# A two-layer ReGLU MLP on one core: x through a DRAM copy and transposing loads, weights in smaller loads, warm-up matmuls ahead

## The chip, the cores and the metric

One core of one Trainium2 chip runs the kernel. The metric is the device time in microseconds (us). Engines are named as the profile names them: PE is TensorE (PEld its weight loads), DVE VectorE, ACT ScalarE, POOL GpSimd, SP SyncE. POOL and SP issue the DMAs; POOL's queue is q0, SP's is q1.

## The reference

```python
def reference(x, w1, w2):          # x [16, 256, 512], w1 [512, 4096], w2 [2048, 512], all fp32
    h = x @ w1
    gate, value = np.split(h, 2, axis=-1)
    h = np.maximum(gate, 0) * value
    return (h @ w2).astype(np.float32)
```

## The kernel before

The 16 x 256 rows of x are 4096 tokens, cut into 8 blocks of 512 (TPB). Blocks are worked in pairs, so there are four passes. All matrix products run in bf16; the weights are cast from fp32 in the DMA that loads them, stay in SBUF for the whole run (w1_sb, w2_sb), and are loaded once, by POOL.

A block needs xT, its x transposed so that the 512 input features lie on the partitions (four slabs of 128, k = 0 to 3). prep_xT makes it. For blocks 0 and 1 (fast_start) SP loads four pieces of 128 tokens in fp32 into x_stage, which has four buffers (L69), an engine that the planner picks casts each to bf16 (L70), TensorE transposes 128 x 128 tiles by a matmul against ident into a PSUM tile ptr (L80), and VectorE copies a finished ptr to xT (L88). For blocks 2 to 7 POOL issues one cast load per block instead of the four pieces (L74); the transposes are the same, 16 a block.

mm1_reglu_pass runs over j, the 16 column tiles of the hidden layer, and inside it over the two blocks of the pair: four matmuls of 512 columns into pv (value half of w1, L113), four into pg (gate half, L121), then ScalarE copies pv to vb (L129) and VectorE forms max(pg, 0) * vb as a slice of h2T (L130). That is 256 matmuls a pass. mm2_pass makes eight output tiles of 128 tokens in a pass, each from 16 matmuls (L145); ScalarE copies the PSUM tile po to ob, of which there are four buffers (L153), and SP stores it (L155). That is 128 matmuls a pass, and none of a pass's mm2 can begin before its h2T slices are there.

w1 is loaded in eight chunks of 512 columns, gate and value halves in turn (L95), each one DMA over all four k; w2 in four groups of four k-tiles (L101). They are traced after the preparation of blocks 0 and 1.

The order of instructions on each engine is fixed when the kernel is built. A planner walks the traced program with a machine model, takes what is ready by the model, and prefers what was traced first; what it puts in a queue is executed in that order, and a head that waits holds the rest of its queue back. The preparation of the next pair is traced ahead of a pass (L171), so the planner may put its transposes among the matmuls of the pass before. Semaphores and buffer reuse are handled by the same layer. At launch, instructions of the launch code (L196, L207) stand around those of the kernel.

Of the kernel before, what the change touches and what calls it, by code (L numbers as in the profile page):

```python
# [10 lines left out]
@with_exitstack  # L11
def kernel(
    ctx: ExitStack,
    tc: tile.TileContext,
    x: bass.AP,
    w1: bass.AP,
    w2: bass.AP,
    out: bass.AP,
):
    nc = tc.nc  # L20
    P = 128
    FP32 = mybir.dt.float32
    BF16 = mybir.dt.bfloat16
    AX = mybir.AluOpType

    x2 = x.flatten_outer_dims()
    out2 = out.flatten_outer_dims()
    M, D = x2.shape
    D_w, H2 = w1.shape
    H, DO = w2.shape  # L30
    assert D_w == D and H2 == 2 * H

    TPB = 512
    NB = M // TPB
    PAIR = 2
    NP = NB // PAIR
    KD = D // P
    NJ = H // P
    KH = H // P
    TS = TPB // P  # L40
    assert NB % PAIR == 0

    consts = ctx.enter_context(tc.tile_pool(name="consts", bufs=1))
    wpool = ctx.enter_context(tc.tile_pool(name="wpool", bufs=1))
    xT_pool = ctx.enter_context(tc.tile_pool(name="xT_pool", bufs=4))
    stage = ctx.enter_context(tc.tile_pool(name="stage", bufs=4))
    h2_pool = ctx.enter_context(tc.tile_pool(name="h2_pool", bufs=4))
    out_pool = ctx.enter_context(tc.tile_pool(name="out_pool", bufs=4))
    psum_mm1 = ctx.enter_context(tc.tile_pool(name="psum_mm1", bufs=2, space=bass.MemoryType.PSUM))
    psum_mm2 = ctx.enter_context(tc.tile_pool(name="psum_mm2", bufs=2, space=bass.MemoryType.PSUM))  # L50
    psum_tr = ctx.enter_context(tc.tile_pool(name="psum_tr", bufs=2, space=bass.MemoryType.PSUM))

    ident = consts.tile([P, P], BF16, name="ident")
    make_identity(nc, ident)

    w1_sb = wpool.tile([P, KD, H2], BF16, name="w1_sb")
    w2_sb = wpool.tile([P, KH, DO], BF16, name="w2_sb")

    w1_r = w1.rearrange("(po pi) f -> pi po f", pi=P)
    w2_r = w2.rearrange("(po pi) f -> pi po f", pi=P)  # L60

    def prep_xT(tb, fast_start):
        x_bf = stage.tile([P, TS, D], BF16, tag="x_bf", name="x_bf", bufs=3)
        if fast_start:
            for t in range(TS):
                tok0 = tb * TPB + t * P
                x_stage = stage.tile([P, D], FP32, tag="x_stage", name="x_stage",
                                     bufs=4)
                nc.sync.dma_start(out=x_stage, in_=x2[tok0:tok0 + P, :])  # L69
                nc.any.tensor_copy(out=x_bf[:, t, :], in_=x_stage)  # L70
        else:
            src = x2[tb * TPB:(tb + 1) * TPB, :].rearrange(
                "(t pi) d -> pi t d", pi=P)
            nc.gpsimd.dma_start(out=x_bf, in_=src)  # L74

        xT = xT_pool.tile([P, KD, TPB], BF16, tag="xT", name="xT")
        for k in range(KD):
            ptr = psum_tr.tile([P, TPB], BF16, tag="ptr", name="ptr")
            for t in range(TS):
                nc.tensor.matmul(  # L80
                    ptr[:, t * P:(t + 1) * P],
                    x_bf[:, t, k * P:(k + 1) * P],
                    ident,
                    is_transpose=True,
                    start=(t == 0),
                    stop=(t == TS - 1),
                )
            nc.vector.tensor_copy(out=xT[:, k, :], in_=ptr)  # L88
        return xT

    W1C = 512
    nchunk_half = H // W1C

    def load_w1_chunk(c):
        nc.gpsimd.dma_start(  # L95
            out=w1_sb[:, :, c * W1C:(c + 1) * W1C],
            in_=w1_r[:, :, c * W1C:(c + 1) * W1C],
        )

    def load_w2_group(g, gsize=4):  # L100
        nc.gpsimd.dma_start(  # L101
            out=w2_sb[:, g * gsize:(g + 1) * gsize, :],
            in_=w2_r[:, g * gsize:(g + 1) * gsize, :],
        )

    def mm1_reglu_pass(pass_blocks, xTs, h2Ts):
        for j in range(NJ):
            for bi, tb in enumerate(pass_blocks):
                xT = xTs[bi]
                pg = psum_mm1.tile([P, TPB], FP32, tag="pg", name="pg")  # L110
                pv = psum_mm1.tile([P, TPB], FP32, tag="pv", name="pv")
                for k in range(KD):
                    nc.tensor.matmul(  # L113
                        pv,
                        w1_sb[:, k, (NJ + j) * P:(NJ + j + 1) * P],
                        xT[:, k, :],
                        start=(k == 0),
                        stop=(k == KD - 1),
                    )
                for k in range(KD):  # L120
                    nc.tensor.matmul(  # L121
                        pg,
                        w1_sb[:, k, j * P:(j + 1) * P],
                        xT[:, k, :],
                        start=(k == 0),
                        stop=(k == KD - 1),
                    )
                vb = stage.tile([P, TPB], BF16, tag="vb", name="vb", bufs=4)
                nc.scalar.copy(out=vb, in_=pv)  # L129
                nc.vector.scalar_tensor_tensor(  # L130
                    out=h2Ts[bi][:, j, :],
                    in0=pg,
                    scalar=0.0,
                    in1=vb,
                    op0=AX.max,
                    op1=AX.mult,
                )

    def mm2_pass(pass_blocks, h2Ts):
        for bi, tb in enumerate(pass_blocks):  # L140
            h2T = h2Ts[bi]
            for t in range(TS):
                po = psum_mm2.tile([P, DO], FP32, tag="po", name="po")
                for k in range(KH):
                    nc.tensor.matmul(  # L145
                        po,
                        h2T[:, k, t * P:(t + 1) * P],
                        w2_sb[:, k, :],
                        start=(k == 0),
                        stop=(k == KH - 1),  # L150
                    )
                ob = out_pool.tile([P, DO], FP32, tag="ob", name="ob")
                nc.scalar.copy(out=ob, in_=po)  # L153
                tok0 = tb * TPB + t * P
                nc.sync.dma_start(out=out2[tok0:tok0 + P, :], in_=ob)  # L155

    xT_tiles = {}
    xT_tiles[0] = prep_xT(0, fast_start=True)
    xT_tiles[1] = prep_xT(1, fast_start=True)

    for c in range(nchunk_half):
        load_w1_chunk(c)
        load_w1_chunk(c + nchunk_half)
    for g in range(KH // 4):
        load_w2_group(g)

    for p in range(NP):
        pass_blocks = [p * PAIR + i for i in range(PAIR)]

        next_blocks = [tb + PAIR for tb in pass_blocks if tb + PAIR < NB]  # L170
        for tb in next_blocks:  # L171
            xT_tiles[tb] = prep_xT(tb, fast_start=False)

        xTs = [xT_tiles.pop(tb) for tb in pass_blocks]
        h2Ts = [
            h2_pool.tile([P, KH, TPB], BF16, tag="h2T", name="h2T")
            for _ in pass_blocks
        ]

        mm1_reglu_pass(pass_blocks, xTs, h2Ts)  # L180
        mm2_pass(pass_blocks, h2Ts)


# [28 lines left out]
```

## Time and profile before

| | us |
|---|---|
| median of 6 runs (370.84 to 373.3) | 372.23 |
| the profiled execution | 370.84 |
| its span, first to last instruction | 369.1 |
| PE busy | 345.1 (94%) |
| DVE busy | 102.8 (28%) |
| ACT busy | 98.7 (27%) |
| POOL busy | 14.2 (4%) |
| mean granted TensorE clock | 0.989 |

The busy share of TensorE counts a matmul from its start to its modelled end, so matmuls that overlap in the pipeline, or run slowly, count as busy all the same. The slices of the page cut the span in 40 pieces of 9.2 us; a digit is a busy share in tenths.

### The profile page before, as it was taken

To read this page: it belongs to the slowest core of one execution; us is meant where nothing else is said; L and a number is where in the kernel's file an instruction comes from. 1 tells how busy PE (TensorE), PEld (TensorE's weight loads), DVE (VectorE), ACT (ScalarE), POOL (GpSimd) and SP (SyncE) were. 2 spreads that over 40 slices of the span, in tenths; PEclk is the share of its full clock that TensorE was granted. 3 is DMA by queue.
4 is the path that set the end of the run, shared out by engine and by line. 5 is a ranking of instruction groups with operands and counts; after the bars stand their busy time and mean duration, and the time that the engine had idled before them with its cause. 6 is when DMAs were issued, how large, how long until landed. Compare 5 with 4: busy or idle time off the path is not lost.

```text
span 369.1 us, 4092 instructions
## 1 busy us (share of the span) xinstructions
PE 345.1 (94%) x1664; PEld 160.0 (43%) x1664; DVE 102.8 (28%) x162; ACT 98.7 (27%) x167; POOL 14.2 (4%) x24
## 2 busy tenths in 40 slices
PE   1597399999999999999999999999999999999996
PEld 0343254444445444444445444444444444444442
DVE  1343153441004443442004433442000433432000
ACT  2233023331112333332112333332112333332111
POOL 7220010000000000000000000000000000000000
PEclk9999699999999999999999999999999999999999
DMA  8999980000215000000221000000212000000212
GB/s 200 250 206 207 206 126 2 1 1 30 85 57 113 2 0 2 0 0 7 80 87 57 0 2 2 0 2 0 85 59 85 0 2 0 0 2 0 85 59 87
DMA packets 15283, 20.19 MB, mean 55 GB/s; under 512 B 928, under 2 KB 10144, under 8 KB 15264
## 3 DMA queue, kind: packets, MB, share of 16 engines
q0 software_dynamic: 9504, 9.44, 15.7%
q1 hardware_dynamic: 5760, 10.49, 7.8%
q8 instruction: 13, 0.21, 0.2%
q14 instruction: 6, 0.05, 0.0%
HBM read 20.97 MB, written 8.39 MB: 80 GB/s over the span
## 4 chain that ended last, share of the span: by engine, by line
PE 87%; DMA 10%; POOL 1%; issue 1%; ACT 0%; POOLq 0%; ACTq 0%
PE po L145 30%; PE pg L121 28%; PE pv L113 28%; DMA x_bf<-in_x_dram 6%; DMA w_sb<-in_w_dram 4%; PE ptr L80 2%; POOL w_sb L95 1%; POOL w_sb L101 0%; ACT ob L153 0%; POOL ident masks.py:199 0%; POOL ident masks.py:197 0%; POOLq masks.py:199 0%; ACTq L153 0%; POOLq L196 0%; POOLq L74 0%
## 5 line engine op out<-in xcount | busy, mean ns | idle before, releaser
L121 PE MATMUL pg<-xT,w_sb 128*128 128x512 bf16 x512 | 134.6, 382 | 0.0
L113 PE MATMUL pv<-xT,w_sb 128*128 128x512 bf16 x512 | 133.7, 382 | 0.0
L130 DVE SCALAR_TENSOR_TENSOR h2T<-pg,vb 128x512 bf16<-128x512 f32 x128 | 88.5, 691 | 155.8 <-PE pg L121 154.7
L129 ACT CAST vb<-pv 128x512 bf16<-128x512 f32 x128 | 74.9, 585 | 161.2 <-PE pv L113 161.2
L145 PE MATMUL po<-w_sb,h2T 128*128 128x512 bf16 x512 | 111.2, 379 | 0.0
L145 PEld LDWEIGHTS <-h2T 128*128 128x128 bf16 x512 | 50.1, 98 | 60.4
L121 PEld LDWEIGHTS <-w_sb 128*128 128x128 bf16 x512 | 50.3, 98 | 58.7 <-issue 0.5
L113 PEld LDWEIGHTS <-w_sb 128*128 128x128 bf16 x512 | 50.2, 98 | 58.4
L153 ACT COPY ob<-po 128x512 f32<-128x512 f32 x32 | 18.7, 585 | 95.4 <-PE po L145 95.4
L80 PE MATMUL ptr<-ident,x_bf 128*128 128x128 bf16 x128 | 15.6, 252 | 20.4 <-ACT x_bf L70 9.3
L88 DVE COPY xT<-ptr 128x512 bf16<-128x512 bf16 x32 | 13.4, 424 | 73.8 <-PE ptr L80 73.3
L80 PEld LDWEIGHTS <-x_bf 128*128 128x128 bf16 x128 | 11.5, 114 | 27.4 <-ACT x_bf L70 10.3
L74 POOL DMA_DIRECT2D x_bf<-in_x_dram x6 | 4.4, 741 | 90.5 <-PE pv L113 66.9
L70 ACT CAST x_bf<-x_stage 128x512 bf16<-128x512 f32 x6 | 3.7, 617 | 10.2 <-DMA x_stage<-in_x_dram 10.2
L95 POOL DMA_DIRECT2D w_sb<-in_w_dram x8 | 6.2, 787 | 0.3 <-issue 0.3
L101 POOL DMA_DIRECT2D w_sb<-in_w_dram x4 | 3.0, 742 | 10.1 <-DMA w_sb<-in_w_dram 10.1
L70 DVE CAST x_bf<-x_stage 128x512 bf16<-128x512 f32 x2 | 1.2, 582 | 6.1 <-DMA x_stage<-in_x_dram 6.1
L70 ACT ACT_TABLE_LOAD x1 | 1.3, 1283 | 0.7 <-PEq L196 0.7
masks.py:199 POOL TENSOR_SCALAR_AFFINE_SELECT ident<-ident 128x128 bf16<-128x128 bf16 x1 | 0.3, 304 | 0.1
masks.py:197 POOL MEMSET ident<- 128x128 bf16 x1 | 0.2, 205 | 0.3 <-POOLq L196 0.3
L196 POOL MEMSET const-float32-0.0<- 128x1 f32 x1 | 0.1, 98 | 0.2 <-issue 0.2
L196 POOL MEMSET const-bfloat16-1.0<- 128x1 bf16 x1 | 0.1, 101 | 0.0
(2 smaller groups left out, 0.2 us busy)
## 6 DMA issues: line engine op xcount, KB each, us to landing
out_dram<-ob SPq DMA_DIRECT2D x32, 256.0 KB, 2.0
w_sb<-in_w_dram POOLq DMA_DIRECT2D x12, 512.0 KB, 19.9
x_bf<-in_x_dram POOLq DMA_DIRECT2D x6, 512.0 KB, 13.4
x_stage<-in_x_dram SPq DMA_DIRECT2D x8, 256.0 KB, 6.2
```

What stands on the lines that cost most here:

```text
L70: nc.any.tensor_copy(out=x_bf[:, t, :], in_=x_stage)
L74: nc.gpsimd.dma_start(out=x_bf, in_=src)
L80: nc.tensor.matmul(ptr[:, t * P:(t + 1) * P], x_bf[:, t, k * P:(k + 1) * P], ident, is_transpose=True, start=(t == 0), stop=(t == TS - 1),)
L88: nc.vector.tensor_copy(out=xT[:, k, :], in_=ptr)
L95: nc.gpsimd.dma_start(out=w1_sb[:, :, c * W1C:(c + 1) * W1C], in_=w1_r[:, :, c * W1C:(c + 1) * W1C],)
L101: nc.gpsimd.dma_start(out=w2_sb[:, g * gsize:(g + 1) * gsize, :], in_=w2_r[:, g * gsize:(g + 1) * gsize, :],)
L113: nc.tensor.matmul(pv, w1_sb[:, k, (NJ + j) * P:(NJ + j + 1) * P], xT[:, k, :], start=(k == 0), stop=(k == KD - 1),)
L121: nc.tensor.matmul(pg, w1_sb[:, k, j * P:(j + 1) * P], xT[:, k, :], start=(k == 0), stop=(k == KD - 1),)
L129: nc.scalar.copy(out=vb, in_=pv)
L130: nc.vector.scalar_tensor_tensor(out=h2Ts[bi][:, j, :], in0=pg, scalar=0.0, in1=vb, op0=AX.max, op1=AX.mult,)
L145: nc.tensor.matmul(po, h2T[:, k, t * P:(t + 1) * P], w2_sb[:, k, :], start=(k == 0), stop=(k == KH - 1),)
L153: nc.scalar.copy(out=ob, in_=po)
```

## The change

Blocks 2 to 7 are no longer transposed by TensorE. POOL casts the rows of a pair from x into a bf16 tensor in DRAM, xbf_dram, in one DMA; SP then loads each xT slab from there with a transposing DMA, four per block, traced between a pass's mm1 and its mm2. Blocks 0 and 1 keep their path, with eight x_stage buffers and two x_bf buffers.

The weight loads are cut differently, and their order on POOL is pinned. The first four column tiles of each half of w1 come one by one, 128 columns over all four k (value before gate); the other three chunks of each half come as one DMA per k; w2 comes as 16 DMAs. Between the first pair of loads and the second, POOL copies one column of x_stage 5, the second piece of block 1, so the rest of the loads waits for that piece.

TensorE gets 22 matmuls of ident against a zeroed tile ahead of everything, and nine more, three behind each of the first three transposes of block 1. Their result is not used. keep_in_program_order pins an instruction behind whatever was traced before it on its engine; it holds the warm matmuls and the transposes of k = 0 in their traced order.

```diff
+    NWARM = 22
...
+    xbf_dram = dram.tile([M, D], BF16, name="xbf_dram")
+    stages = []
+    zeros = consts.tile([P, TPB], BF16, name="zeros")
+    nc.vector.memset(zeros, 0.0)
+    warm = psum_mm2.tile([P, DO], FP32, tag="po", name="warm")
+    for i in range(NWARM):
+        tc.keep_in_program_order(
+            nc.tensor.matmul(warm, ident, zeros, start=True, stop=True))
+
+    def prep_xT_pe(tb):
+        x_bf = stage.tile([P, TS, D], BF16, tag="x_bf", name="x_bf", bufs=2)
+        for t in range(TS):
+            tok0 = tb * TPB + t * P
+            x_stage = stage.tile([P, D], FP32, tag="x_stage",
+                                 name="x_stage", bufs=8)
+            stages.append(x_stage)
+            nc.sync.dma_start(out=x_stage, in_=x2[tok0:tok0 + P, :])
+            nc.any.tensor_copy(out=x_bf[:, t, :], in_=x_stage)
...
+                if k == 0:
+                    tc.keep_in_program_order(mm)
+                if tb == 1 and k == 0 and t < TS - 1:
+                    for i in range(3):
+                        tc.keep_in_program_order(
+                            nc.tensor.matmul(warm, ident, zeros, start=True, stop=True))
...
+    def cast_x_to_dram(blocks):
+        lo = blocks[0] * TPB
+        hi = (blocks[-1] + 1) * TPB
+        tc.keep_in_program_order(
+            nc.gpsimd.dma_start(out=xbf_dram[lo:hi, :], in_=x2[lo:hi, :]))
+
+    def prep_xT_dma(tb):
+        xT = xT_pool.tile([P, KD, TPB], BF16, tag="xT", name="xT")
+        rows = slice(tb * TPB, (tb + 1) * TPB)
+        for k in range(KD):
+            nc.sync.dma_start_transpose(
+                xT[:, k, :],
+                xbf_dram[rows, k * P:(k + 1) * P],
+            )
+        return xT
+
+    def load_weights():
+        pin = tc.keep_in_program_order
+        for j in range(4):
+            for half in (1, 0):
+                c0 = (half * NJ + j) * P
+                pin(nc.gpsimd.dma_start(
+                    out=w1_sb[:, :, c0:c0 + P],
+                    in_=w1_r[:, :, c0:c0 + P],
+                ))
+            if j == 0:
+                gate = consts.tile([P, 1], FP32, name="gate")
+                pin(nc.gpsimd.tensor_copy(out=gate, in_=stages[5][:, 0:1]))
+        W1C = 512
+        nchunk_half = H // W1C
+        for c in range(1, nchunk_half):
+            for k in range(KD):
+                pin(nc.gpsimd.dma_start(
+                    out=w1_sb[:, k, c * W1C:(c + 1) * W1C],
+                    in_=w1_r[:, k, c * W1C:(c + 1) * W1C],
+                ))
+            for k in range(KD):
+                cc = c * W1C + H
+                pin(nc.gpsimd.dma_start(
+                    out=w1_sb[:, k, cc:cc + W1C],
+                    in_=w1_r[:, k, cc:cc + W1C],
+                ))
+        for k in range(KH):
+            pin(nc.gpsimd.dma_start(out=w2_sb[:, k, :], in_=w2_r[:, k, :]))
...
     xT_tiles = {}
-    xT_tiles[0] = prep_xT(0, fast_start=True)
-    xT_tiles[1] = prep_xT(1, fast_start=True)
...
+    for tb in range(PAIR):
+        xT_tiles[tb] = prep_xT_pe(tb)
+
+    load_weights()
 
     for p in range(NP):
         pass_blocks = [p * PAIR + i for i in range(PAIR)]
-
         next_blocks = [tb + PAIR for tb in pass_blocks if tb + PAIR < NB]
-        for tb in next_blocks:
-            xT_tiles[tb] = prep_xT(tb, fast_start=False)
+
+        if next_blocks:
+            cast_x_to_dram(next_blocks)
...
         mm1_reglu_pass(pass_blocks, xTs, h2Ts)
+
+        for tb in next_blocks:
+            xT_tiles[tb] = prep_xT_dma(tb)
+
         mm2_pass(pass_blocks, h2Ts)
```

## Rows read from the trace of the kernel before

**Rows 1.** The page: busy tenths, granted clock, DMA share and GB/s in 40 slices of the span.

```profile
PE   1597399999999999999999999999999999999996
...
PEclk9999699999999999999999999999999999999999
DMA  8999980000215000000221000000212000000212
GB/s 200 250 206 207 206 126 2 1 1 30 85 57 113 2 0 2 0 0 7 80 87 57 0 2 2 0 2 0 85 59 85 0 2 0 0 2 0 85 59 87
```

**Rows 2.** The chain that ended last, in order of time: start us, us, what.

```profile
22.65 20.52 DMA x_bf<-in_x_dram
...
85.50 27.63 PE po L145 x128
...
170.22 27.63 PE po L145 x128
...
254.95 27.63 PE po L145 x128
...
337.83 27.64 PE po L145 x128
```

**Rows 3.** Timeline, idle stretch: start us, us, engine, line, op, tiles, count [idle before <-releaser].

```profile
34.52 0.38 PE L121 MATMUL pg<-xT,w_sb 128*128 128x512 bf16 x1
...
43.22 1.04 PE L80 MATMUL ptr<-ident,x_bf 128*128 128x128 bf16 x8 [8.32 <-DMA x_bf<-in_x_dram]
...
44.04 1.06 PE L121 MATMUL pg<-xT,w_sb 128*128 128x512 bf16 x2
```

**Rows 4.** Windows there: us, busy (count) PE, PEld, DVE, ACT, POOL, PEclk, DMA share, GB/s.

```profile
40.50:41.50 1.00, 0.00 (x0) 0.00 (x0) 0.00 (x0) 0.00 (x0) 0.00 (x0) 0.50 1.23 205
...
46.00:46.50 0.50, 0.50 (x5) 0.33 (x4) 0.43 (x1) 0.00 (x0) 0.00 (x0) 0.50 1.08 178
...
47.00:47.50 0.50, 0.50 (x4) 0.20 (x2) 0.50 (x2) 0.00 (x0) 0.42 (x1) 1.00 0.16 27
```

**Rows 5.** Timeline, the head (0 to 21 us).

```profile
0.74 8.66 SPq L69 DMA_DIRECT2D x_stage<-in_x_dram  x8
1.26 0.87 POOL L95 DMA_DIRECT2D w_sb<-in_w_dram  x1 [0.32 <-issue]
2.23 0.30 POOL masks.py:199 TENSOR_SCALAR_AFFINE_SELECT ident<-ident 128x128 bf16<-128x128 bf16 x1
...
3.45 0.62 ACT L70 CAST x_bf<-x_stage 128x512 bf16<-128x512 f32 x1 [1.43 <-DMA x_stage<-in_x_dram]
...
15.27 0.62 ACT L70 CAST x_bf<-x_stage 128x512 bf16<-128x512 f32 x1 [0.80 <-DMA x_stage<-in_x_dram]
...
16.02 0.63 PE L121 MATMUL pg<-xT,w_sb 128*128 128x512 bf16 x1
...
18.58 0.99 PE L113 MATMUL pv<-xT,w_sb 128*128 128x512 bf16 x2
...
20.07 0.74 POOL L101 DMA_DIRECT2D w_sb<-in_w_dram  x1 [1.80 <-DMA w_sb<-in_w_dram]
```

**Rows 6.** The view of tile x_stage: its loads from issue to landing.

```profile
DMA to landing us min/median/max: 2.7/6.2/7.5
```

**Rows 7.** Timeline, TensorE, start of the second mm1 pass.

```profile
112.96 0.61 PE L80 MATMUL ptr<-ident,x_bf 128*128 128x128 bf16 x8
...
116.10 0.38 PE L80 MATMUL ptr<-ident,x_bf 128*128 128x128 bf16 x4
116.32 0.38 PE L121 MATMUL pg<-xT,w_sb 128*128 128x512 bf16 x1
```

**Rows 8.** The page: DMA issues (count, KB each, median us to landing).

```profile
out_dram<-ob SPq DMA_DIRECT2D x32, 256.0 KB, 2.0
...
x_bf<-in_x_dram POOLq DMA_DIRECT2D x6, 512.0 KB, 13.4
```

**Rows 9.** The page: DMA queue q0 (packets, MB, share of 16 engines).

```profile
q0 software_dynamic: 9504, 9.44, 15.7%
```

More of the change, by code (lines that the diff above doesn't have):

```diff
@@ L60 @@
     w2_r = w2.rearrange("(po pi) f -> pi po f", pi=P)
[L62 to L74, printed above, removed]
+    xbf_dram = dram.tile([M, D], BF16, name="xbf_dram")
[15 more added lines that the diff above has]
+            nc.any.tensor_copy(out=x_bf[:, t, :], in_=x_stage)
         xT = xT_pool.tile([P, KD, TPB], BF16, tag="xT", name="xT")
@@ L87, in prep_xT @@
                 )
+                if k == 0:
[4 more added lines that the diff above has]
+                            nc.tensor.matmul(warm, ident, zeros, start=True, stop=True))
             nc.vector.tensor_copy(out=xT[:, k, :], in_=ptr)
         return xT
[L91 to L104, printed above, removed]
+    def cast_x_to_dram(blocks):
[12 more added lines that the diff above has]
+        return xT
@@ L157 @@
     xT_tiles = {}
-    xT_tiles[0] = prep_xT(0, fast_start=True)
-    xT_tiles[1] = prep_xT(1, fast_start=True)
[L161 to L165, printed above, removed]
+    for tb in range(PAIR):
+        xT_tiles[tb] = prep_xT_pe(tb)
+    load_weights()
     for p in range(NP):
```

5 lines of the change are left out of this document (3 added, 2 removed).

## The prediction

> **What bounds the kernel now.** Read the slices first [rows 1]: TensorE is at 9 from the seventh slice to the last, so after about 60 us nothing but its own stream sets the time; what can be saved lies in the first six slices, where its digits dip and the DMA engines are at 8 or 9. Then the chain in order of time [rows 2]: each mm2 pass is one piece of 128 matmuls in 27.63 us, 0.216 us per matmul with no gap. The last mm1 pass runs from 254.95 + 27.63 = 282.58 to 337.83, 55.25 us, again 0.216 for each of 256. The second runs from 85.50 + 27.63 = 113.13 to 170.22, 57.09 us: 1.84 more, the price of 32 transposes in full stream. The third is the same (170.22 + 27.63 to 254.95).
>
> So let S be the moment at which the first mm1 pass would have begun had its 256 matmuls run without a gap. Before, it ended at 85.50, so S = 85.50 - 55.25 = 30.25. That number is the whole matter, and the next views split it. Around the idle stretch [rows 3] the last matmul starts at 34.52 and the next work, transposes of the third block, at 43.22: 8.32 us in which TensorE waits for the cast load of x. That load was issued at 22.65 and landed 20.5 us later [rows 2], since it queued behind the weights. The windows [rows 4] show what the wait costs afterwards: granted clock 0.50 (1.2 GHz) from 40.50 on, still 0.50 at 46.00 to 46.50, 1.00 (2.4 GHz) from 47.00. In that stretch two 512-column matmuls take 1.06 [rows 3]. The head [rows 5] shows one alone in 0.63 at 16.02, although the slices grant it a 9: the duration, not that digit, tells that the head runs at 1.2 GHz, and 1.06 - 0.63 = 0.43 is the step from one to the next there, against 0.216. The pair at 18.58 takes 0.99, a little less than 1.06, so the rise falls into its end, near 19.4, 3.4 us after gapless work began at 16.02; the second rise, about 46.7, came 3.5 us after 43.22. The eight pieces of x land one by one, the first cast at 3.45, the last at 15.27 [rows 5], and TensorE waits for each.
>
> **The change part by part.** With no stall after the first pass the new span is S + 55.25 + 27.63 + 3 x (55.25 + 27.63) + the tail. The tail is 369.1 - (337.83 + 27.64) = 3.63 and untouched, so the span is S + 335.2. Around the span lie 370.84 - 369.1 = 1.74, and the median shown is 372.23 - 370.84 = 1.39 above the profiled run; so the median is S + 338.3.
>
> *Transposes of blocks 2 to 7.* All 96 leave TensorE. Those of the second and third pass were worth 2 x 1.84 = 3.7 us. Those of the first pass leave with the idle stretch, whose parts (8.32 idle, 1.84 of work, some 2 at the low clock) are in S. 24 PSUM copies leave VectorE too, which never ended a wait of the dense stretch: nothing.
>
> *Warm-up.* ident was done at 2.23 + 0.30, behind a weight issue of 0.87 at 1.26 [rows 5]. The first weight issue is now pinned behind it, so ident is ready near 1.26 + 0.30 = 1.6. The 22 matmuls start there: 3.5 us at 0.43 is 8, the other 14 take 14 x 0.216 = 3.0, so they end at 8.2. No transpose may pass them. If the clock never rose they would end at 1.6 + 22 x 0.43 = 11.1. The zeroing ahead of them on VectorE is shorter than the wait for ident.
>
> *x of blocks 0 and 1.* Eight buffers instead of four: SP issues all eight loads without waiting for a cast. Only 0.52 MB of weights (fp32) goes out beside them until the sixth piece is in. From the third slice to the fifth the engines write 206 GB/s in bf16 [rows 1], so read 412 GB/s in fp32, which is one 2 KB packet per 79.5 ns and engine, and 0.64 us for a piece of 262 KB. The first piece is in 2.7 after its issue at 0.74 [rows 5, 6], at 3.4; seven more are 4.5, the weights beside them 1.3 by bytes: the last at 9.2. If the 64 small packets per engine of these weights cost as much as large ones, they are 5.1, and the last is in at 13.0.
>
> *TensorE's order.* After the warm-up come the 32 transposes and 9 more warm matmuls (9 x 0.216 = 1.94). A row of 32 transposes with matmuls between took from 112.96 to 116.5, 0.44 for each group of four [rows 7], and cost 1.84 net. If x is there, S = 8.2 + 1.84 + 1.94 = 12.0. If the last piece is at 13.0, then its cast (0.62), the transpose behind it and three groups 0.44 apart follow, some 2.2, less the eight matmuls of block 0 that fit between (1.7): S = 13.5.
>
> *The gate and the weights.* POOL's copy of x_stage 5 is the added wait. Behind it on POOL stand every weight load but the first two, then the casts of x to DRAM; TensorE's j = 1 waits for the two next. The sixth piece is in after five of those seven steps, at 7.5 to 10.3; I take 7.5. With the copy (say 0.2, against 0.30 for the larger select that ends ident [rows 5]), one issue (0.8) and 1.0 to the first packet, an estimate from the 2.7 less a piece's 0.64 and the way back, data moves at G = 9.5. Each j of 1 to 3 needs 1024 packets of 512 B read and 256 B written, 64 per engine; the next chunk, j = 4 to 7, needs 64 of the old size, 5.1 us. With p the time of a small packet this chunk is in at G + 192p + 5.1 and is wanted at S + 4 x 3.45 = S + 13.8. So S is at least 9.5 + 192p - 8.7. No packet of that kind is in the trace: by bytes p is 20 ns and the bound is 4.6, no bound; at the price of a large packet, 79.5, S = 16.1. The later chunks come every 5.9 us (8 issues at 0.74 [rows 5]) and serve 13.8 us each, so they are early. The large packet is the nearest row and a ceiling as far as bytes go, so S lies between 12.0 and 16.1; I take the middle, 14.0 (p = 69).
>
> *x through DRAM.* POOL's 46 issues behind the gate end near 7.8 + 46 x 0.75 = 42; the packets (512 per engine, up to 79.5 each) end near 50. A cast of 1024 rows is 64 packets per engine, 5.1 us, so blocks 2 and 3 are in DRAM at 55 to 57. SP then issues 8 transposing loads of 128 KB, and the first pass ends its mm2 at 14 + 82.9 = 97. The cover is some 38 us, 4.7 for each. No transposing load is in the trace: the 256 KB store lands in 2.0, the cast load of 512 KB in 13.4 under load [rows 8]; 512 packets of 256 B at 79.5 over 16 engines are 2.5. I take 2.5, 20 in all, hidden. The other end is packets of one element, 65536 x 79.5 / 16 = 326 us a load. Output stores stand behind them on SP, and ScalarE's four output buffers would feel that only past the cover. The Trainium skill's "DMA: Bandwidth & Descriptors" (Latency and other measured facts) gives 261 GB/s for transposing DMAs, an estimate of 0.5 us each and 4 in all, hidden as well; no run here has shown it.
>
> **Sum.** S falls from 30.25 to 14.0, 16.25 us, and 3.7 leave with the transposes: 19.9 less, 350.9 against 370.84 for the profiled run, 352.3 as a median. Likeliest range 350 to 354.5.
>
> **The rivals.**
> *Small packets bind (0.18).* With p from 85 to 159 ns, a packet that costs more than a large one, TensorE waits in j = 1 to 4. Mean duration of a q0 packet is already 0.157 x 16 x 369.1 / 9504 = 97.6 ns with two queues sharing [rows 9]; there S = 9.5 + 18.7 - 8.7 = 19.5, 357.8. At twice 79.5, S = 31.3: 369.6, no gain. Against it: nothing in the trace says that a small packet costs more than a large one. The Trainium skill's page named above (Specifications) says that transfers under 512 B become a read, a modify and a write; that rule is this rival, since the chunks write 256 B, and nothing in the trace decides it.
>
> *The head stays (0.08).* The planner fixes TensorE's order; in the head it put a matmul among transposes that waited for x [rows 5]. If the clock stays low over the 31 warm matmuls, S = 1.6 + 31 x 0.43 + 3.7 (twice 1.84) = 18.6: 356.9. Against it: both rises before came 3.4 to 3.5 us after gapless work began.
>
> *The detour is late (0.06), slower.* If a transposing load takes t, the second pass starts late by 8t - 38. Past t = 6.8 us (19 GB/s) that eats the 16.25, and 3.7 more at t = 7.2; at t = 13.4, the slow row, it starts 69 late and the median is 421, with later passes covered by 82.9 each up to t = 10. For it: two trips through memory and an operation never seen here. Against it: by bytes the store's row gives 1.0 a load, almost five times less than the cover.
>
> *The stall only moves (0.04).* The change would not do what it says if the planner put matmuls of the second pass, or of j = 4, where their inputs are late, as it did at 34.9. An idle stretch like the old one with its clock costs 8.3 + 2: 362.6.
>
> That leaves 0.64 for the forecast. Faster by over 0.5% (about the least that a measurement of this kernel can tell, 1.9 us) is all but the late detour and the far end of the packets: 0.92. Within 0.5%: 0.02. Slower: 0.06. The range runs from S = 9.5, all weights and x at byte rate with matmuls filling every gap, 347.8, to S = 25 (p about 126), 363.
>
> **What would show it.** A first mm2 pass that starts at S + 55.25 = 69, not 85.5, and no wait of TensorE on a DMA after it: right. mm1 passes of 55.25 each: the transposes are gone. Matmuls 0.216 apart before 8 us: the warm-up works. TensorE waiting for the weights in j = 1 to 4: the packets bind. The first transposing load landing after 97, or TensorE waiting for xT at a pass's start: the detour is late, and the prediction wrong.

## The result, and the profile after

The changed kernel takes 350.32 us (median of 8 runs, 349.72 to 350.64); the kernel before, with more runs beside it, 371.88. The ratio is 0.9421, interval 0.9406 to 0.9435. The prediction's sum was 352.3, its range 347.8 to 363. The profiled execution took 350.21, its span is 348.4.

The page of the changed kernel, the same four lines as [rows 1], each slice now 8.7 us:

```profile
PE   8999999999999999999999999999999999999995
...
PEclk9999999999999999999999999999999999999999
DMA  8999999753200000034210000001120000000121
GB/s 212 149 188 200 201 249 169 111 94 130 79 32 0 0 2 0 0 67 146 90 62 0 0 1 2 1 0 62 62 89 32 0 0 2 0 0 31 61 90 62
```

TensorE is at 8 in the first slice and at 9 from the second to the last but one, and no slice has a granted clock below 9; the dips up to 50 us are gone (that the first matmuls run slowly is not in that digit, here as before). The DMA engines are busy longer: the casts and transposing loads of x stand at 41 to 77 us, beside matmuls.

The chain that ended last, in order of time (start, duration, what), answers to [rows 2]:

```profile
1.36 7.22 PE warm L73 x22
...
68.06 27.63 PE po L190 x128
...
150.94 27.63 PE po L190 x128
...
316.70 27.64 PE po L190 x128
```

The old chain held two long waits on DMAs, the cast load of [rows 2] and, ahead of it, one on weights:

```profile
3.95 15.84 DMA w_sb<-in_w_dram
```

Neither is in the new chain; it starts with the warm-up matmuls and is TensorE from there to its last matmul, but for 0.44 of VectorE in the head. The first mm2 pass begins at 68.06 instead of 85.50, so S, the moment at which a gapless first mm1 pass would have begun, is 68.06 - 55.25 = 12.81 (before 30.25). Each later mm1 pass takes 150.94 - 68.06 - 27.63 = 55.25, the gapless value, where before the second and third took 57.09.

Timeline of the head (start, duration, engine, line, operation, tiles, count, idle time and what ended it), to be read beside [rows 5]:

```profile
1.36 7.22 PE L73 MATMUL warm<-zeros,ident 128*128 128x512 bf16 x22 [1.36 <-POOL ident masks.py:199]
...
7.65 0.62 ACT L83 CAST x_bf<-x_stage 128x512 bf16<-128x512 f32 x1 [3.77 <-DMA x_stage<-in_x_dram]
...
8.42 0.61 PE L89 MATMUL ptr<-ident,x_bf 128*128 128x128 bf16 x8
...
9.66 0.18 POOL L133 COPY gate<-x_stage 128x1 f32<-128x1 f32 x1 [6.55 <-DMA x_stage<-in_x_dram]
...
11.46 0.62 ACT L83 CAST x_bf<-x_stage 128x512 bf16<-128x512 f32 x1 [0.28 <-DMA x_stage<-in_x_dram]
...
13.72 0.81 PE L166 MATMUL pg<-xT,w_sb 128*128 128x512 bf16 x3
...
16.09 1.03 PE L158 MATMUL pv<-xT,w_sb 128*128 128x512 bf16 x4
```

The 22 warm matmuls take 7.22. A last one at full speed takes 0.38, so the 21 steps between starts are 6.84: 11 of 0.43 and 10 of 0.216, and the clock rose some 4.7 us after 1.36. The fourth piece of x is in at 7.65, its cast ends at 8.27, block 0's transposes begin at 8.42. The gate's copy starts at 9.66, the last cast at 11.46. From 13.72 on matmul follows matmul, among them those of j = 1 at 16.09, with no wait for a weight.

The windows (us, busy time and count of PE, PEld, DVE, ACT, POOL, clock, DMA share, GB/s written), for four kinds of transfer: mostly x in fp32, the small weight loads alone, the larger ones, the transposing loads. Behind them stands what SP's queue, q1, moved in the first of them (packets, MB, share), which is x:

```profile
8.00:10.00 2.00, 1.71 (x21) 1.23 (x20) 1.01 (x3) 1.25 (x3) 0.34 (x2) 1.00 1.13 323
12.00:16.00 4.00, 4.00 (x30) 2.19 (x28) 2.30 (x5) 1.23 (x3) 4.00 (x8) 1.00 1.51 143
25.00:35.00 10.00, 10.00 (x48) 4.55 (x47) 4.15 (x6) 3.50 (x6) 8.15 (x16) 1.00 1.24 201
62.00:76.00 14.00, 14.00 (x67) 6.36 (x65) 2.77 (x4) 3.51 (x6) 0.00 (x0) 1.00 0.56 104
...
q1 hardware_dynamic: 321, 0.58, 82.2%
```

The issues on the page (count, KB each, median us to landing), SP's queue in order of time, and the first copy of an output tile by ScalarE:

```profile
w_sb<-in_w_dram POOLq DMA_DIRECT2D x48, 128.0 KB, 4.9
...
xT<-xbf_dram SPq DMA_TRANSPOSE x24, 2.9
```

```profile
51.14 26.11 SPq L116 DMA_TRANSPOSE xT<-xbf_dram  x16
77.35 19.36 SPq L200 DMA_DIRECT2D out_dram<-ob  x8
```

```profile
71.55 0.58 ACT L198 COPY ob<-po 128x512 f32<-128x512 f32 x1 [3.73 <-PE po L190]
```

A transposing load lands in 2.9 (median; the first ones take up to 9.7). SP issues sixteen of them from 51.14 on, blocks 4 and 5 with blocks 2 and 3, and only then, at 77.35, the first store, though its data was ready at 71.55 + 0.58 = 72.1.

### The profile page after: what moved, and what is told of

Its sections match the earlier page's. It is cut to its first block, busy times and chain, and to the rows that moved or that the text cites. A ratio compares the mean times of both kernels' runs of the same rounds, so it can differ in the third digit from the quotient of the medians.

```text
span 348.4 us, 3993 instructions
## 1 busy us (share of the span) xinstructions
PE 342.7 (98%) x1599; PEld 155.6 (45%) x1599; DVE 92.9 (27%) x139; ACT 98.6 (28%) x167; POOL 29.6 (8%) x58
## 4 chain that ended last, share of the span: by engine, by line
PE 98%; ACT 0%; POOL 0%; DVE 0%; issue 0%; POOLq 0%; ACTq 0%
PE pg L166 32%; PE po L190 32%; PE pv L158 32%; PE warm L73 2%; PE warm L102 1%; PE ptr L89 1%; ACT ob L198 0%; DVE xT L103 0%; POOL ident masks.py:199 0%; POOL ident masks.py:197 0%; POOLq masks.py:199 0%; ACTq L198 0%; POOLq L241 0%
## 5 line engine op out<-in xcount | busy, mean ns | idle before, releaser
L158 PE MATMUL pv<-xT,w_sb 128*128 128x512 bf16 x512 | 131.7, 379 | 0.0
L166 PE MATMUL pg<-xT,w_sb 128*128 128x512 bf16 x512 | 131.6, 380 | 0.0
L149 POOL DMA_DIRECT2D w_sb<-in_w_dram x16 | 8.5, 528 | 1.9 <-issue 0.2
L73 PE MATMUL warm<-zeros,ident 128*128 128x512 bf16 x22 | 7.2, 505 | 1.4 <-POOL ident masks.py:199 1.4
L138 POOL DMA_DIRECT2D w_sb<-in_w_dram x12 | 6.4, 554 | 2.1 <-DMA w_sb<-in_w_dram 1.4
L144 POOL DMA_DIRECT2D w_sb<-in_w_dram x12 | 6.4, 544 | 1.5 <-DMA w_sb<-in_w_dram 0.8
L127 POOL DMA_DIRECT2D w_sb<-in_w_dram x8 | 6.1, 780 | 0.2 <-issue 0.2
L73 PEld LDWEIGHTS <-ident 128*128 128x128 bf16 x22 | 2.6, 124 | 5.5 <-issue 3.0
L103 DVE COPY xT<-ptr 128x512 bf16<-128x512 bf16 x8 | 3.2, 422 | 4.4 <-PE ptr L89 4.1
L89 PE MATMUL ptr<-ident,x_bf 128*128 128x128 bf16 x32 | 3.2, 219 | 0.3 <-DVE xT L103 0.3
L89 PEld LDWEIGHTS <-x_bf 128*128 128x128 bf16 x32 | 2.4, 97 | 1.6 <-issue 0.4
L102 PE MATMUL warm<-zeros,ident 128*128 128x512 bf16 x9 | 2.2, 379 | 0.0
L110 POOL DMA_DIRECT2D xbf_dram<-in_x_dram x3 | 1.5, 502 | 0.4 <-issue 0.2
```

The costliest lines, as they stand in the source:

```text
L73: nc.tensor.matmul(warm, ident, zeros, start=True, stop=True))
L89: mm = nc.tensor.matmul(ptr[:, t * P:(t + 1) * P], x_bf[:, t, k * P:(k + 1) * P], ident, is_transpose=True, start=(t == 0), stop=(t == TS ...
L127: pin(nc.gpsimd.dma_start(out=w1_sb[:, :, c0:c0 + P], in_=w1_r[:, :, c0:c0 + P],))
L138: pin(nc.gpsimd.dma_start(out=w1_sb[:, k, c * W1C:(c + 1) * W1C], in_=w1_r[:, k, c * W1C:(c + 1) * W1C],))
L144: pin(nc.gpsimd.dma_start(out=w1_sb[:, k, cc:cc + W1C], in_=w1_r[:, k, cc:cc + W1C],))
L149: pin(nc.gpsimd.dma_start(out=w2_sb[:, k, :], in_=w2_r[:, k, :]))
```

## The experiments

S in each is the start of the first mm2 pass less 55.25.

**The detour alone.** The kernel before with blocks 2 to 7 by the DRAM copy; head and weights as they were.

```diff
-        for tb in next_blocks:
-            xT_tiles[tb] = prep_xT(tb, fast_start=False)
+        if next_blocks:
+            cast_x_to_dram(next_blocks)
...
+        for tb in next_blocks:
+            xT_tiles[tb] = prep_xT_dma(tb)
         mm2_pass(pass_blocks, h2Ts)
```

> The kernel before with the detour alone: blocks 2 to 7 by the cast to DRAM and transposing loads, head and weights as before. If the terms add up, the stall (8.3), its transposes (1.8), the low clock after it (2.0) and the two later groups of transposes (3.7) leave: 371.9 - 15.8 = 356.1, first mm2 pass near 73.4. If the weights in large loads come too late once the stall no longer hides them: 358 to 362. If the head's changes carry most of the gain: 365 or more.

Measured: 356.46, ratio 0.9582 (0.9554 to 0.961). The chain after:

```profile
74.75 27.63 PE po L164 x128
```

The last cast of x, in its timeline:

```profile
16.46 0.62 ACT L89 CAST x_bf<-x_stage 128x512 bf16<-128x512 f32 x1 [0.71 <-DMA x_stage<-in_x_dram]
```

S = 19.50; the terms gave 18.1. The detour takes 15.3 of the 21.6 us off, where the terms said 15.8. The last cast of x starts at 16.46 here and at 15.27 in the kernel before, which is most of the difference. The large weight loads do not come late: TensorE waits for none of them.

**TensorE transposes put back.** The changed kernel with the old preparation of blocks 2 to 7, its cast loads pinned behind the weights: prep_xT_old is one cast load on POOL and 16 transposes on TensorE.

```diff
-        if next_blocks:
-            cast_x_to_dram(next_blocks)
+        for tb in next_blocks:
+            xT_tiles[tb] = prep_xT_old(tb)
...
-        for tb in next_blocks:
-            xT_tiles[tb] = prep_xT_dma(tb)
```

> Blocks 2 to 7 go back to cast loads and TensorE transposes, the loads pinned behind the weights on POOL; head and weights stay as in the changed kernel. The order of TensorE has the transposes of blocks 2 and 3 about 85 matmuls into the first pass, at some 31 us, and the cast load of block 2 is issued near 41 and lands near 50. If the detour is what takes the stall away: an idle stretch of about 20 us, 2 for the clock, 5.5 for 96 transposes: 375 to 380. If the smaller weight loads and the shorter head were enough: 350.3 + 5.5 = 356.

Measured: 375.11, ratio 1.0088 (1.0064 to 1.0113), slower than the kernel before. Its timeline where TensorE stands still:

```profile
29.57 0.59 PE L178 MATMUL pv<-xT,w_sb 128*128 128x512 bf16 x2
...
40.98 2.24 POOL L126 DMA_DIRECT2D x_bf<-in_x_dram  x3
...
47.83 1.03 PE L131 MATMUL ptr<-ident,x_bf 128*128 128x128 bf16 x8 [17.67 <-DMA x_bf<-in_x_dram]
```

TensorE stops near 30.16 and goes on at 47.83, 17.67 idle, until the cast load issued at 40.98 is in. The stall is 9.3 longer than before, half of it from either end: TensorE reaches the transposes 4.7 earlier (30.16, before 34.52 + 0.38 = 34.90), and the load, again behind all weights, is in 4.6 later (47.8, before 43.2). The shorter head and the smaller loads thus don't remove the stall, and taking the transposes out of TensorE's queue does. A third way, the same cast loads ahead of w2, which is not needed before the first mm2, was not tried.

**Transposing loads twice.** After each, the same slab goes once more into a scratch tile that nothing reads.

```diff
                 xbf_dram[rows, k * P:(k + 1) * P],
             )
+            for _ in range(1):
+                extra = stage.tile([P, TPB], BF16, tag="extra", name="extra", bufs=8)
+                nc.sync.dma_start_transpose(
+                    extra,
+                    xbf_dram[rows, k * P:(k + 1) * P],
+                )
         return xT
```

> Each transposing load is followed by the same load into a scratch tile; SP's order then has 40 of them ahead of the first store, 16 in the changed kernel. By the prediction's account only xT of the second pass counts: its last load is issued by 51 + 16 x 1.63 = 77 and needed at 95.7, so no change, 350.3. If the stores behind them on SP are the nearer limit: the first goes out at 51 + 40 x 1.63 = 116, four ob and two po buffers let TensorE go to 68 + 6 x 3.45 = 89, so it idles some 29 us and loses 2 to the clock: about 381.

Measured: 375.71, ratio 1.012 (1.0084 to 1.0156). The timeline:

```profile
81.81 7.50 PE L196 MATMUL po<-w_sb,h2T 128*128 128x512 bf16 x34
...
108.46 13.51 SPq L206 DMA_DIRECT2D out_dram<-ob  x8
110.84 1.28 ACT L204 COPY ob<-po 128x512 f32<-128x512 f32 x2 [27.81 <-DMA out_dram<-ob]
111.47 9.46 PE L196 MATMUL po<-w_sb,h2T 128*128 128x512 bf16 x32 [22.16 <-ACT ob L204]
```

The stores come out at 108.46, and the two lines behind show what that does: ScalarE waited 27.81 for a store to free an output buffer, TensorE 22.16 for ScalarE to free a PSUM tile. That is the second case of the expectation; its 29 idle were too many since most of the loads went out 1.3 us apart, not the 1.63 taken from the changed kernel (a mean that holds waits). The cover that ends first is thus not the next pass's xT but the store queue. TensorE stopped at 81.81 + 7.50 = 89.3, and went on 3.0 after the first store's issue (108.46 to 111.47); so a first store issued up to about 86 costs nothing, and in the changed kernel it goes out at 77.35, some 9 us earlier.

**No warm-up.** The 31 warm matmuls are left out.

```diff
-    for i in range(NWARM):
-        tc.keep_in_program_order(
-            nc.tensor.matmul(warm, ident, zeros, start=True, stop=True))
...
-                if tb == 1 and k == 0 and t < TS - 1:
-                    for i in range(3):
-                        tc.keep_in_program_order(
-                            nc.tensor.matmul(warm, ident, zeros, start=True, stop=True))
```

> The 31 warm-up matmuls are left out, nothing else. If they matter by the clock: the transposes and the first matmuls run at 1.2 GHz until some 3.5 to 4.7 us after gapless work begins near 12, which costs about half of that, 2 us, and two early matmuls of block 0: about 352.5, with 512-column matmuls 0.43 apart up to about 16 us. If they only stand in the way of block 0's transposes (they end at 8.58, the cast before those transposes at 8.27): 350.0, no change.

Measured: 352.34, ratio 0.9476 (0.9452 to 0.95), 2.0 above the changed kernel; its first mm2 starts at 69.81, S = 14.56. The timeline:

```profile
10.83 0.62 ACT L77 CAST x_bf<-x_stage 128x512 bf16<-128x512 f32 x1 [0.30 <-DMA x_stage<-in_x_dram]
...
12.86 1.06 PE L148 MATMUL pv<-xT,w_sb 128*128 128x512 bf16 x2
...
16.12 1.03 PE L148 MATMUL pv<-xT,w_sb 128*128 128x512 bf16 x4
```

The last cast starts at 10.83, earlier than in the changed kernel, yet the pair of matmuls at 12.86 takes 1.06, the slow step; full speed (four in 1.03) is there at 16.12. So the warm-up is worth its 2 us by the clock.

**No warm matmuls in the middle.** Only the nine go.

```diff
-                if tb == 1 and k == 0 and t < TS - 1:
-                    for i in range(3):
-                        tc.keep_in_program_order(
-                            nc.tensor.matmul(warm, ident, zeros, start=True, stop=True))
```

> Only the nine warm matmuls between block 1's first transposes are left out. They fill a wait (10.2 to 12.3 us; the last cast of x ends at 12.08): no change, within 0.5 us of 350.3. If the clock needs them: it falls or rises late and 512-column matmuls after 12 us are 0.43 apart, 352.

Measured: 350.0 (0.9422, 0.9392 to 0.9451), first mm2 at 68.04: no change. They fill a wait and keep nothing warm that would have cooled.

**No gate.**

```diff
-                gate = consts.tile([P, 1], FP32, name="gate")
-                pin(nc.gpsimd.tensor_copy(out=gate, in_=stages[5][:, 0:1]))
```

> POOL's copy of x_stage 5 is left out, so the weight loads go out without waiting. If the order of arrival sets the head: the last four pieces of x share the DMA engines with weights, 1.6 us a piece instead of 1.0, the last cast ends near 14.7 instead of 12.08, and the time is about 353. If the engines move the same bytes and only the total counts: 350.3, no change.

Measured: 350.65 (0.9428, 0.9409 to 0.9446), not told from the changed kernel; first mm2 at 68.82, 0.8 later in the profiled execution. The timeline:

```profile
12.40 0.62 ACT L83 CAST x_bf<-x_stage 128x512 bf16<-128x512 f32 x1 [0.28 <-DMA x_stage<-in_x_dram]
```

The last cast starts at 12.40 instead of 11.46, 0.9 later and not the 2.6 expected: the weight loads that now run beside x take less from it than was put. By the medians the order that the gate sets is worth next to nothing.

**Large weight loads.** The twelve loads of before behind the new head, the gate after the first two.

```diff
-        for j in range(4):
-            for half in (1, 0):
-                c0 = (half * NJ + j) * P
+        W1C = 512
+        nchunk_half = H // W1C
+        for c in range(nchunk_half):
+            for cc in (c, c + nchunk_half):
...
```

> The weights come in the twelve large loads of before, gate after the first two. If small loads help by putting less beside x and letting j = 0 start early: the first two chunks are 2.1 MB of reads beside the x pieces, x and w1 for j = 0 are in near 14 to 15, about 352.5. If packets of 256 B written are dear, as the rival in the prediction had it: faster than 350.3. If the size of the loads doesn't matter: 350.3.

Measured: 358.83, ratio 0.964 (0.9614 to 0.9667), 8.5 above the changed kernel; 2 were expected. The timeline, a line of the chain that ended last, then windows with the granted clock (last but two):

```profile
15.52 0.61 PE L148 MATMUL pv<-xT,w_sb 128*128 128x512 bf16 x1 [4.86 <-DMA w_sb<-in_w_dram]
...
16.88 1.49 PE L102 MATMUL warm<-zeros,ident 128*128 128x512 bf16 x3
```

```profile
2.33 13.14 DMA w_sb<-in_w_dram
```

```profile
12.00:13.00 1.00, 0.00 (x0) 0.00 (x0) 0.00 (x0) 0.29 (x1) 1.00 (x2) 0.50 1.17 268
20.00:21.00 1.00, 1.00 (x4) 0.37 (x3) 0.00 (x0) 0.00 (x0) 0.14 (x1) 0.50 1.25 208
22.00:24.00 2.00, 2.00 (x17) 1.17 (x16) 1.45 (x4) 0.59 (x1) 0.54 (x1) 1.00 1.24 207
```

x is late (its last cast starts at 14.32), and the first matmul waits 4.86 for w1 until 15.52; in that wait the clock has gone to 0.50, which the warm-up had raised, and the next matmuls run at 0.43 a step, the nine warm ones (three in 1.49) now among them and in the way, until past 20. The first mm2 begins at 76.94, S = 21.69. That is even later than in the detour alone (19.50), which has no warm matmuls: here the warm-up, which no work followed for 4.86 us, bought nothing. Part of the lateness may be order and not size: the edit loads the gate chunk ahead of the value chunk, while TensorE's queue begins with the value half (pv), whose load, the second, was in only at 2.33 + 13.14 = 15.47. In the detour alone, with the same chunks, it begins with the gate half. The two were not separated.

**x by cast loads.** x of blocks 0 and 1 in bf16 on POOL's queue, in line with the weights; 13 warm matmuls, no gate.

```diff
-            nc.sync.dma_start(out=x_stage, in_=x2[tok0:tok0 + P, :])
-            nc.any.tensor_copy(out=x_bf[:, t, :], in_=x_stage)
-
+            tc.keep_in_program_order(nc.gpsimd.dma_start(
+                out=x_bf[:, t, :], in_=x2[tok0:tok0 + P, :]))
...
+    x_bf0 = load_x(0)
+    load_w1_tile(0)
+    xT_tiles[0] = prep_xT_pe(x_bf0)
+    x_bf1 = load_x(1)
     load_weights()
+    xT_tiles[1] = prep_xT_pe(x_bf1)
```

> x of blocks 0 and 1 comes in bf16 by eight cast loads on POOL in one queue with the weights (x block 0, w1 for j = 0, x block 1, the rest), 13 warm-up matmuls, no gate, no casts by ScalarE or VectorE. If the head is bound by the arrival of x in fp32 (pieces about 1.0 us apart): cast pieces at 0.64 apart are all in near 9.5, dense work starts about 2 to 3 us earlier, 347.5 to 348.5. If the warm-up and the clock bind: no change, 350.3. If POOL's issue of every load in one line binds: slower, 351 to 353.

Measured: 348.83 (348.73 to 349.04), ratio 0.9383 (0.9361 to 0.9405): faster than the changed kernel by 1.5, less than hoped. The timeline and the chain:

```profile
1.45 2.28 POOL L79 DMA_DIRECT2D x_bf<-in_x_dram  x4
...
9.99 0.23 PE L96 MATMUL ptr<-ident,x_bf 128*128 128x128 bf16 x1 [0.56 <-DMA x_bf<-in_x_dram]
...
11.34 0.40 PE L96 MATMUL ptr<-ident,x_bf 128*128 128x128 bf16 x4 [0.25 <-DMA x_bf<-in_x_dram]
```

```profile
67.15 27.63 PE po L185 x128
```

Block 1's pieces still come at 9.99 to 11.34, each waited for; S = 11.90. Of the versions that were run it has the lowest median. The edit changes several things at once: the gate and the nine matmuls moved the median by 0.3 each above, the nine fewer warm matmuls ahead were not tried alone.

**x on both queues.** Block 0 in fp32 by SP, block 1 by cast loads on POOL, behind the first weights (mixed_x) or ahead of them (mixed_x_first).

```diff
-    for tb in range(PAIR):
-        xT_tiles[tb] = prep_xT_pe(tb)
-
+    x_bf0 = load_x_sp(0)
+    load_w1_tile(0)
+    xT_tiles[0] = prep_xT_pe(x_bf0)
+    x_bf1 = load_x(1)
     load_weights()
+    xT_tiles[1] = prep_xT_pe(x_bf1)
```

This is mixed_x against the changed kernel; in mixed_x_first the line with load_x(1) stands behind the first one.

> As cast_x, but block 0 of x comes in fp32 on SP's queue with casts by ScalarE or VectorE, while POOL's queue loads w1 for j = 0, then block 1 as four cast loads, then the rest. In cast_x the first mm2 pass began at 67.15 and TensorE waited for pieces of block 1 until 12. If two queues from the first microsecond shorten the head: block 0 transposed from 6.5 on, block 1 in by 9 to 10, first mm2 at 64.5 to 66, median 346.5 to 347.7. If the bytes on the engines bind whatever the queue: 348.8.

> As mixed_x, with block 1's cast loads ahead of w1 for j = 0 on POOL. Both blocks are in near 7 to 8, but the first matmul, which stands among block 0's last transposes, waits for w1 until 9 or so, and those behind it with it: if w1 then binds, 347.5 to 348.5, slower than mixed_x; if x binds, 346.5, faster than mixed_x.

> The changed kernel unaltered, beside the two on the same chip: 350.3.

Measured beside each other: 349.32 (0.9402, 0.9375 to 0.9428), 351.34 (0.943, 0.9406 to 0.9454), and 350.34 (0.942, 0.9406 to 0.9434) for the changed kernel. A second queue brings nothing over cast_x that the medians can tell, which agrees with the account by bytes; that the bytes bind was not tried by itself. mixed_x_first is 2.8 us above the upper end of what was expected; its timeline and two windows:

```profile
8.21 0.23 PE L106 MATMUL ptr<-ident,x_bf 128*128 128x128 bf16 x1 [2.24 <-DVE x_bf L90]
...
9.74 0.45 PE L106 MATMUL ptr<-ident,x_bf 128*128 128x128 bf16 x5 [1.30 <-ACT x_bf L90]
...
11.11 0.46 PE L163 MATMUL pv<-xT,w_sb 128*128 128x512 bf16 x1 [0.24 <-DMA w_sb<-in_w_dram]
...
11.79 0.63 PE L163 MATMUL pv<-xT,w_sb 128*128 128x512 bf16 x1
```

```profile
10.00:13.00 3.00, 2.46 (x19) 1.55 (x17) 1.71 (x5) 0.00 (x0) 2.99 (x6) 0.72 1.81 178
...
11.00:11.50 0.50, 0.39 (x3) 0.24 (x4) 0.33 (x1) 0.00 (x0) 0.50 (x1) 0.80 1.81 179
```

Neither of the two expected ends binds: TensorE waits 0.24 for w1. It waits 2.24 and 1.30 for the last pieces of block 0 from SP, now beside block 1's loads, with two short pieces of work between and after, and meets its first matmul at 11.11 as the clock falls (granted 0.80 from 11.0 to 11.5, 0.50 after); at 11.79 a matmul takes 0.63. The single executions spread with the clock: 348.88 at a mean granted clock of 0.998, 351.76 at 0.990 (mixed_x: 348.36 at 1.000, 351.96 at 0.990).

## Why the prediction was right

*What bounds, and the size of the stall.* Right, and shown: the detour alone takes 15.3 where its terms, stall, clock and two groups of transposes, were 15.8, and with the transposes back on TensorE the stall returns at 17.67. The later passes are 55.25 each, as worked out. (In [rows 1] TensorE is at 9 from the sixth slice on, not the seventh, and at 6 in the last; nothing hangs on it.) The other 6.1 us, from 356.46 to 350.32, are the head's, and they are not split to the end: the warm-up is worth 2.0, the gate next to nothing, the large weight loads cost 8.5 but with the order of the halves in it, and the eight x_stage buffers were not tried by themselves.

*The sum.* S was put at 14.0 and is 12.81, 1.2 less. The tail grew from 3.63 to 348.4 - (316.70 + 27.64) = 4.06, around the span lie 350.21 - 348.4 = 1.81 instead of 1.74, and the runs' median is 0.11 above the profiled run instead of 1.39: 352.3 - 1.2 + 0.4 + 0.1 - 1.3 = 350.3.

*The weights' bound on S* is the term that was mis-sized. It took p, the time of a packet of 512 B read and 256 B written, as 69 ns, which is what puts S in the middle between 12.0 and 16.1. From 12 to 16 us the engines wrote 143 GB/s of such packets and of nothing else, 143 / 16 = 8.9 GB/s each, 256 B in 28.6 ns, near the 20 by bytes; in mixed_x_first, from 10 to 13 us, it was 178 GB/s, 23 ns. With p = 28.6 the bound falls away, TensorE waits for no weight, and the rival of dear packets goes with it. By the Trainium skill's "DMA: Bandwidth & Descriptors" (Specifications) a transfer under 512 B becomes a read, a modify and a write; if that happens here, its price is within the 8.6 ns above the byte rate. The same term was wrong the other way too: the gate's copy came at 9.66, inside the 7.5 to 10.3 given, of which 7.5 was taken; that puts G at 11.6. With p = 69 the bound would then have been 11.6 + 13.2 - 8.7 = 16.1; the small packets were cheap enough to hide it.

*x of blocks 0 and 1* was put too low: 0.64 a piece at the rate of cast loads. From 8 to 10 us the engines wrote 323 GB/s, where the larger cast loads read 2 x 201 from 25 to 35; 0.58 MB of that was x, 290 GB/s or 0.90 a piece, and the casts of the last five pieces start 0.89 to 1.08 apart. The last piece came at 11.4, inside the 9.2 to 13.0 given. The path that sets S was the one by the warm-up, x and the transposes, 12.0 to 13.5 in the prediction, and 12.81 lies in it. That 14.0, the middle between that path and a bound that did not bind, came so near is in part luck; that the stall, the transposes and the clock leave is not.

*The warm-up* ended at 8.58 instead of 8.2, since the clock rose after 4.7 and not after 3.5, and is worth 2.0; that the clock would rise by it was right. The gate, to which the change gives a line of its own, is worth 0.3 by the medians, which the intervals do not tell from nothing.

*The detour's cover* was wrong in its place, though nothing came of it. The prediction let 8 loads be issued ahead of the second pass, 38 us of cover, and said that the stores behind them would be felt only past that. The planner put 16 ahead of the first store, and transposes_twice shows that stores give out first. The price of a load was right in size: 2.9 to landing against 2.5, and 1.3 of SP's time. The Trainium skill's page just named (Latency and other measured facts) gives 261 GB/s for transposing DMAs. A load of 131 KB each 1.3 us is 101 GB/s here, but that is the pace at which SP let them out: from 62 to 76 us the DMA share was 0.56, so the engines had room, and what they could do was not measured. No load ended a wait of TensorE.

*The rivals.* That the head stays slow needs the clock to stay low over the warm-up; coarse_weights is how that looks, by another road. The late detour did not occur: the first transposing load went out at 51.14 and was in by 61, the sixteenth went out before 77.35, and xT was wanted at 95.7. That the stall only moves did not occur: the chain after the head is TensorE alone.

## What to carry to other kernels

In a stream that is gapless later on, read the saving from the head and from stalls as one number, the start that a gapless first pass would have had, and price each early resource by its own row. Work that depends on a late load and stands in the middle of the busiest engine's queue can be moved to another engine, as here; shortening what comes before it lengthens the wait, as pe_transposes shows. When loads are added to a queue, count all that the planner puts ahead of what was there, and look at how many buffers stand between that queue and the busy engine.

## What the runs showed of the hardware

The clock's rise is not fixed from run to run. The same 22 matmuls from 1.36 on stand at the head of seven profiles, and took from 6.21 (pe_transposes) to 7.85 (no_mid_warm):

```profile
1.36 6.21 PE L73 MATMUL warm<-zeros,ident 128*128 128x512 bf16 x22 [1.36 <-POOL ident masks.py:199]
...
1.36 7.85 PE L73 MATMUL warm<-zeros,ident 128*128 128x512 bf16 x22 [1.36 <-POOL ident masks.py:199]
```

That is about 6 to 14 of 21 steps at 1.2 GHz, a rise 2.6 to 5.9 us after work began. The two rises of the kernel before, 3.4 and 3.5, were two points of a wider spread.

The clock fell again near 11 us in coarse_weights and mixed_x_first, after short pieces of work with idle between, where in the kernel before it had stayed up until some 5 us into an idle stretch: TensorE was idle there from 34.90 on, and the windows are

```profile
39.50:40.00 0.50, 0.00 (x0) 0.00 (x0) 0.00 (x0) 0.00 (x0) 0.00 (x0) 0.86 1.24 207
40.00:40.50 0.50, 0.00 (x0) 0.00 (x0) 0.00 (x0) 0.00 (x0) 0.00 (x0) 0.50 1.24 207
```

A transposing load held SP's queue for 1.26 us (median), against 0.40 for an x load on the same queue in the kernel before. A weight load's issue on POOL took 0.53 for 128 packets and 0.77 for 512.
